# A fixed VectorE order and a fixed DMA order in the middle of a hybrid decoder layer

## The chip, the cores and the metric

The kernel runs on one core of a Trainium2 chip. The metric is the device time of one execution in microseconds (us). The engines of the core work side by side: TensorE (PE in the profile; PEld is its weight load), VectorE (DVE), ScalarE (ACT), GpSimd (POOL) and SyncE (SP), whose queue issues nearly all DMAs here. Each engine takes its instructions in the order in which the program gives them, and an instruction can wait for a semaphore of another engine.

## The reference, cut to what matters

The layer has a token-mixing part with three branches, then cross-attention and an MLP; the sequence and the width are both 1024. The change lies in the end of the token mixing.

```python
u = h @ w_in
dq, dk, dv, rq, rk, rv, rg, lx, ly, gates = split(u)
od  = diff_attention(...)                      # branch 0
o_r = silu(rg) * group_norm(retention(...))    # branch 1
hl  = rg_lru_branch(lx, ...)                   # branch 2
o_l = hl * gelu(ly)
g = sigmoid(gates)
merged = g[0]*(od @ w_branch[0]) + g[1]*(o_r @ w_branch[1]) + g[2]*(o_l @ w_branch[2])
x = x + merged @ w_out

def rg_lru_branch(xb):                         # per block of 128 channels
    xc = causal_conv(xb, width 4) + conv_b
    r, i = sigmoid(xc @ w_a + b_a), sigmoid(xc @ w_x + b_x)
    log_a = -8 * r * softplus(-lam)
    b = sqrt(-expm1(2*log_a)) * i * xc
    h[t] = exp(log_a[t]) * h[t-1] + b[t]
```

All is in float32; the kernel reaches that on TensorE by splitting each operand into an upper and a lower part and multiplying three times.

## The kernel before, in words

**Number format.** `split` (line 68) writes the upper part of an operand with a ScalarE copy (line 70) and the lower part with a subtraction on VectorE or GpSimd (line 71). `mm3` (lines 57 to 61) makes three matmuls of the upper and lower parts.

**Products.** The projections of the gates, of the silu input `rg`, of the LRU inputs and of the three branches are done with Strassen's scheme in Winograd's form: a pair of output tiles (two units of 128 channels, all 1024 positions) takes seven products of twelve 128x512 matmuls. `product` (line 1158) issues one product into one of six PSUM buffers (`p6`, line 751) and then whatever combination of products has become possible: `u2`, `u3` and the update behind `c22` (lines 1182, 1184, 1187) on VectorE, and `emit` for a finished quarter of the output. The order of the seven is `ORDER`, (1, 2, 6, 7, 5, 4, 3).

**Weights.** `ahead` (line 1143) runs `prep` some three products in front of the use: `pair_load` loads the two raw weight tiles (line 1128) into the pool `stage` of three buffers, or for odd pairs partly into a fixed tile, `left` (line 1117) makes the four sums of the scheme on VectorE, and `pair_unit` splits each left operand.

**Jobs.** `h_products` (line 664) runs 23 pairs one after the other: four `rg` pairs, eight `lru` pairs (at even places from 2 to 16) and eleven `gate` pairs. A `gate` pair stores its raw values (line 707) into the DRAM tensor `gsp`. An `rg` pair loads the retention output, applies silu and multiplies (lines 709 to 713). An `lru` pair ends in the convolution of four VectorE steps (lines 613 and 615, all of them behind its sixth product); in the next pair follow the split of the result (`xcs`) behind the sixth product and behind the seventh `lru_gate` (line 623): twelve matmuls, sigmoids into the tiles r and g, GpSimd's multiply (634), tanh, exp and square root (635 to 637) and four VectorE steps, of which line 640 is the scan, and the store of the block (642).

**Right operands of the branches.** `o_sums` (line 755) loads two rows of a branch's input into the same tiles r and g, makes four subtractions on VectorE (765) and stores the sums (767). The list `sums` says behind which pair each of the twelve turns stands, one or two to a pair.

**Branches.** `branch` (line 812) runs four pairs for each branch, the last two interleaved. Its `emit` loads the gate tile (822), takes the sigmoid (823), loads the partial sum of the branch before (826), does two or three VectorE steps (828, 829, 831) and stores the sum (833) or, for the last rows of the last branch, splits it for `w_out`. `load_blocks` and `fill_block` load and split the next branch's right operands (791); at the end of the third branch the first half of `w_o` is loaded in four pieces through one tile `wst` (880) and split, and the last block of the merged rows is filled.

**What sets the order.** The instructions are written in program order, but a planner sorts those of each engine by dependencies, priorities and its own durations. `after(key, ins)` (line 74) fixes the order of the instructions that carry the same key, without a semaphore; `wdma` and `hdma` are such keys for weight and block loads.

## Time and profile before

| | us |
|---|---|
| median of 3 runs | 2422.93 (2420.59 to 2424.95) |
| the profiled execution | 2424.15 |
| its span, first to last instruction | 2422.4 |
| TensorE busy | 2319.7 (96%) |
| VectorE busy | 1888.0 (78%) |
| ScalarE busy | 1041.4 (43%) |
| GpSimd busy | 955.9 (39%) |

The order of the stages on the span: retention and attention up to about 745 us, `h_products` from there to about 1252, the branches to about 1505, `w_out` behind them, then cross-attention and MLP. A row of the profile names the line, the engine, the operation, the tile written and those read; "x" gives a count, then come busy time, mean time of one in ns, and the idle time of the engine in front of it with what ended it. A row of waits gives who waited, for whom, us in total, times and the longest. A row of a stretch gives its bounds and length, then the busy time and number of instructions of PE, PEld, DVE, ACT and POOL, the granted TensorE clock (1.00 is full), the busy share of the DMA engines and GB/s. Matmuls are pipelined and their ends are modelled, so that their busy times overlap; starts are counted instead.

### The profile page before, as it was taken

Reading aid. Unit: us, or ns where it says so; the run is one execution under the profiler, and the core shown is the slowest. Engines: PE = TensorE matmul, PEld = TensorE weight load, DVE = VectorE, ACT = ScalarE, POOL = GpSimd, SP = SyncE. Lnnn points to the kernel's source line nnn. Section 1 sums busy time; section 2 is a strip of 40 time slices with the busy share of each in tenths; the row PEclk is TensorE's granted clock in tenths of the full one; section 3 lists DMA queues with packets and bytes.
Section 4 is the critical chain, followed back from the end, with each engine's and each line's share of the span. In section 5 each row is a group of like instructions: output and inputs, shape, how many; then the busy total and the mean of one; then the engine's idle time right before and its main releaser. Section 6 shows DMA issues by size and latency. Waiting matters only on the chain. (4 is left out here: it accounts for less than half of the span.)

```text
span 2422.4 us, 31108 instructions
## 1 busy us (share of the span) xinstructions
PE 2319.7 (96%) x11156; PEld 1913.1 (79%) x11156; DVE 1888.0 (78%) x2909; ACT 1041.4 (43%) x1817; POOL 955.9 (39%) x621
## 2 busy tenths in 40 slices
PE   9999999999999998999999988999989999899998
PEld 7888878888887876777887767778768888788886
DVE  7677487878797788798787898344788888788896
ACT  5443355555555543554354444135442222343333
POOL 1122212222215444455431223034155555598863
PEclk9999999999999999999999999999999999999999
DMA  5222122222215354543576687343225443744341
GB/s 173 81 87 70 58 70 60 64 71 70 62 49 180 127 162 162 174 134 136 178 266 240 228 287 239 105 146 119 97 83 183 152 144 135 254 167 166 121 165 70
DMA packets 135994, 335.12 MB, mean 138 GB/s; under 512 B 17040, under 2 KB 27281, under 8 KB 135840
## 3 DMA queue, kind: packets, MB, share of 16 engines
q1 hardware_dynamic: 135264, 331.30, 41.4%
q8 instruction: 89, 1.46, 0.2%
q10 hardware_dynamic: 576, 1.84, 0.2%
q14 instruction: 65, 0.53, 0.1%
HBM read 227.64 MB, written 97.05 MB: 134 GB/s over the span
## 5 line engine op out<-in xcount | busy, mean ns | idle before, releaser
L59 PE MATMUL ps<-block,wu 128*128 128x512 f32 x1428 | 568.6, 398 | 27.2 <-DVE sf L1187 10.4
L61 PE MATMUL ps<-block,wu 128*128 128x512 f32 x1428 | 565.3, 396 | 10.2 <-DVE wu L71 10.2
L60 PE MATMUL ps<-block,wu 128*128 128x512 f32 x1428 | 561.9, 394 | 0.8 <-DVE block L71 0.8
L71 POOL TENSOR_TENSOR wu<-st,wu 128x512 fp32r<-128x512 f32 x144 | 227.3, 1585 | 303.4 <-ACT wu L70 290.4
L59 PEld LDWEIGHTS ps<-block,wu 128*128 128x128 f32 x1428 | 272.4, 191 | 89.0 <-DVE sf L1187 11.3
L61 PEld LDWEIGHTS ps<-block,wu 128*128 128x128 f32 x1428 | 271.2, 190 | 75.1 <-DVE wu L71 13.3
L60 PEld LDWEIGHTS ps<-block,wu 128*128 128x128 f32 x1428 | 271.8, 190 | 61.0 <-DVE block L71 1.3
L70 ACT CAST wu<-st 128x512 fp32r<-128x512 f32 x240 | 141.9, 620 | 210.1 <-DVE st L1117 94.1
L71 POOL TENSOR_TENSOR w<-st,w 128x1024 fp32r<-128x1024 f32 x50 | 124.6, 2501 | 176.7 <-ACT w L70 176.5
L59 PE MATMUL ps<-wu,hu 128*128 128x512 f32 x456 | 179.4, 394 | 8.0 <-ACT wu L70 4.2
L60 PE MATMUL ps<-wu,hu 128*128 128x512 f32 x456 | 178.9, 392 | 0.9 <-POOL wu L71 0.8
L61 PE MATMUL ps<-wu,hu 128*128 128x512 f32 x456 | 178.6, 392 | 0.0
L71 POOL TENSOR_TENSOR wu<-sf,wu 128x512 fp32r<-128x512 f32 x63 | 122.2, 1954 | 131.9 <-ACT wu L70 95.8
L1273 DVE TENSOR_TENSOR acc<-acc,ps 128x512 f32<-128x512 f32 x184 | 118.1, 679 | 19.8 <-PE ps L61 19.4
L71 DVE TENSOR_TENSOR hu<-sth,hu 128x1024 fp32r<-128x1024 f32 x53 | 118.1, 2231 | 14.3 <-ACT hu L70 13.6
L466 ACT ACTIVATE p<-sc,mx 128x256 f32<-128x256 f32 (+7 forms) x128 | 94.8, 742 | 69.9 <-DVE mx L463 50.1
L71 DVE TENSOR_TENSOR wu<-st,wu 128x512 fp32r<-128x512 f32 x96 | 91.1, 960 | 30.9 <-ACT wu L70 30.8
L59 PEld LDWEIGHTS ps<-wu,hu 128*128 128x128 f32 x456 | 86.3, 189 | 28.7 <-ACT wu L70 4.6
L59 PE MATMUL psk<-block,w 128*128 128x512 f32 x256 | 101.6, 397 | 0.0
L60 PEld LDWEIGHTS ps<-wu,hu 128*128 128x128 f32 x456 | 86.3, 189 | 19.3 <-POOL wu L71 1.3
L61 PE MATMUL psk<-block,w 128*128 128x512 f32 x256 | 101.2, 395 | 0.0
L60 PE MATMUL psk<-block,w 128*128 128x512 f32 x256 | 100.8, 394 | 0.0
(383 smaller groups left out, 5627.4 us busy)
## 6 DMA issues: line engine op xcount, KB each, us to landing
sth<-h SPq DMA_DIRECT2D x53, 512.0 KB, 3.2
st<-in_w SPq DMA_DIRECT2D x32, 512.0 KB, 4.2
h<-hab SPq DMA_DIRECT2D x32, 512.0 KB, 2.8
w<-in_w SPq DMA_DIRECT2D x8, 2048.0 KB
block<-oTs SPq DMA_DIRECT2D x24, 512.0 KB, 5.8
sgb<-gsp SPq DMA_DIRECT2D x48, 256.0 KB, 5.3
gsp<-l SPq DMA_DIRECT2D x44, 256.0 KB, 2.8
acc<-y SPq DMA_DIRECT2D x40, 256.0 KB, 2.9
```

Source lines behind the costliest of these rows:

```text
L59: nc.tensor.matmul(ps, lhsT=lhs.hi, rhs=rhs.hi, start=start, stop=False)
L60: nc.tensor.matmul(ps, lhsT=lhs.hi, rhs=rhs.lo, start=False, stop=False)
L61: nc.tensor.matmul(ps, lhsT=lhs.lo, rhs=rhs.hi, start=False, stop=stop)
L70: ins = self.nc.scalar.copy(dst.hi, src)
L71: self.lo_ins = (lo_engine or self.nc.vector).tensor_tensor(dst.lo, src, f32(dst.hi), op=ALU.subtract)
L466: nc.scalar.activation(p[:, 0:n], sc[:, 0:n], AF.Exp, bias=mx, accum_out=l)
L1273: v.tensor_tensor(acc[k][:, st, :], acc[k][:, st, :], ps, op=ALU.add)
```

## The change

1. For pairs 2 to 20 of `h_products` each VectorE instruction is tied to the one before it in the program (`InOrder`), so that VectorE's order there is the program's.
2. The LRU work is cut into steps, at most one behind a product: the convolution behind the sixth and seventh product of its pair and the first two of the next, the split behind the third, the gate behind the fifth, and the four steps of the scan behind products two to five of the pair after that.
3. `o_sums` becomes a generator: loads behind the fifth product, its subtractions one to three at a time behind later products. The multiply and store of an `rg` quarter come two products later.
4. In the branches the loads of weights, blocks, gates and partial sums and the stores go in one order on SyncE (`one_queue`). Three gate tiles are loaded ahead, two are already through the sigmoid; partial sums are loaded ahead; each store is issued one emit later.
5. The weights of the next branch's first pair are loaded earlier, into a tile of the branch pool (`room`). `w_o` comes in two loads of two pieces, split behind products 7 and 3; the last block of the merged rows is split inside `w_out`.

No arithmetic is added or left out.

```diff
+class InOrder:
+    def __getattr__(self, name):
+        def issue(*args, **kw):
+            ins = getattr(self.engine, name)(*args, **kw)
+            if self.kernel.in_order:
+                self.kernel.after("dve", ins)
+            return ins
+        return issue
...
     def after(self, key, ins):
+        if self.one_queue and key in ("wdma", "hdma"):
+            key = "sp"
...
+    def lru_scan(self, n, c, step):
+        v, xc, gy, (r, g) = self.nc.vector, c["xc"], c["gy"], c["rg"]
+        if step == 0:
+            v.scalar_tensor_tensor(g, r, 1.0, g, op0=ALU.add, op1=ALU.mult)
+        elif step == 1:
+            v.tensor_tensor(xc, xc, g, op=ALU.mult)
+        elif step == 2:
+            v.tensor_tensor_scan(g, r, xc, 0.0, op0=ALU.mult, op1=ALU.add)
+        else:
+            v.tensor_tensor(gy, gy, g, op=ALU.mult)
+            self.nc.sync.dma_start(self.olT[n * P:(n + 1) * P, :], gy)
...
+            in_bw = bool(turns) and p >= m + 2
+            if in_bw:
+                at = 6
             if k == at and p == (turns or [p])[0] and q < len(pairs):
-                self.pair_load(q, *pairs[q])
+                self.pair_load(q, *pairs[q], self.bw.tile([P, 2, D], F32, tag="wst", name="wst") if in_bw else None)
...
-            if kind == "lru" and k == self.ORDER[5]:
-                self.lru_conv(n, c, sp)
...
+            if lru(p - 2) and 0 < at < 5:
+                self.lru_scan(jobs[p - 2][1], cs[p - 2], at - 1)
+            if lru(p) and at > 4:
+                self.lru_conv(n, c, sp, at - 5)
+            if lru(p - 1):
+                if at < 2:
+                    self.lru_conv(jobs[p - 1][1], cs[p - 1], sp, at + 2)
+                elif at == 2:
                     self.lru_split(cs[p - 1])
-                elif k == self.ORDER[6]:
+                elif at == 4:
                     self.lru_gate(jobs[p - 1][1], cs[p - 1], sp, sps)
-            if k == self.ORDER[2]:
-                for i, q in sums.get(p, ()):
-                    self.o_sums(i, q, sp)
+            if p in sums and at == 4:
+                self.steps = itertools.chain.from_iterable(self.o_sums(i, q, sp) for i, q in sums[p])
+                next(self.steps)
+            if p == m - 3 and p in sums:
+                count = {5: 2, 6: 2}.get(at, 0)
+            elif p in sums:
+                count = len(sums[p]) * (at == 6)
+            elif p < m - 2:
+                count = {0: {1: 1, 2: 3}, 1: {1: 1}, 2: {1: 1, 2: 2}, 3: {2: 2}}.get(at, {}).get(len(sums.get(p - 1, ())), 0)
...
+        def fetch():
+            if self.sg_line:
+                r, sl, i = self.sg_line.popleft()
+                sg = bw.tile([P, HB], F32, tag="sg", name="sgb", bufs=4)
+                self.after("sp", nc.sync.dma_start(sg, self.gsp[i * D + r * P:i * D + (r + 1) * P, sl]))
+                self.sgs.append([sg, False])
+            if self.pv_line and (len(self.sgs) > 2 or not self.sg_line):
+                at, r, sl = self.pv_line.popleft()
+                pv = None
+                if at > 0:
+                    pv = bw.tile([P, HB], F32, tag="pv", name="pv", bufs=3)
+                    self.after("sp", nc.sync.dma_start(pv, self.acc[at - 1][r * P:(r + 1) * P, sl]))
+                self.pvs.append(pv)
+            for g in [g for g in list(self.sgs)[:2] if not g[1]]:
+                g[1] = True
+                nc.scalar.activation(g[0], g[0], AF.Sigmoid)
+
+        def store(last=1):
+            while len(self.stores) > last:
+                self.after("sp", nc.sync.dma_start(*self.stores.popleft()))
...
-            if k in (7, 5, 3, 4):
-                if k in (7, 3):
-                    w.append(self.block(self.slotB))
-                q = units % 2
-                self.split(w[-1][:, 2 * q:2 * q + 2, :], wst, (v, nc.gpsimd)[q])
-                units += 1
+            if k in (7, 3):
+                w.append(self.block(self.slotB))
+                for q in range(2):
+                    self.split(w[-1][:, 2 * q:2 * q + 2, :], wst[:, q].rearrange("p (k c) -> p k c", k=2), (v, nc.gpsimd)[q])
+            if k in (1, 7):
+                wst = bw.tile([P, 2, D], F32, tag="wst", name="wst")
+                for q in range(2):
+                    self.after("sp", nc.sync.dma_start(wst[:, q], self.a["w_o"][0, (0 if k == 1 else 2) + q]))
...
+                    if half == 0 and j == 1 and cb == 1:
+                        self.fill_block()
```

More of the change, by code (lines that the diff above doesn't have):

```diff
@@ L1 @@
 import collections
+import itertools
 from contextlib import ExitStack
@@ L667, in h_products @@
             pairs += [(b[p], [a["w_br"][i * 8 + 2 * p + e] for e in range(2)]) for p in range(4)]
+        puts = collections.deque()
         def prep(p, k):
@@ L716, in run @@
             self.product(k, c, H, psum or self.p6(sps), emit)
-            if kind == "lru" and k == self.ORDER[5]:
-                self.lru_conv(n, c, sp)
             if p == 1 and k == 3:
                 self.softplus()
-            if p > 0 and jobs[p - 1][0] == "lru":
-                if k == self.ORDER[5]:
+            for x in puts:
+                x[0] -= 1
+            while puts and puts[0][0] == 0:
+                puts.popleft()[1]()
+            at = self.ORDER.index(k)
+            lru = lambda q: 0 <= q < m and jobs[q][0] == "lru"
@@ L730, in h_products @@
+            if p == m - 3 and p in sums:
[4 more added lines that the diff above has]
+                count = {0: {1: 1, 2: 3}, 1: {1: 1}, 2: {1: 1, 2: 2}, 3: {2: 2}}.get(at, {}).get(len(sums.get(p - 1, ())), 0)
+            else:
+                count = 0
+            for _ in range(count):
+                next(self.steps)
         for p in range(2):
@@ L832, in emit @@
             if nxt is not None or n < 4:
-                nc.sync.dma_start(self.acc[order][rows, sl], o)
+                self.stores.append((self.acc[order][rows, sl], o))
             else:
                 self.split(mT[j][1][:, n % 4, :], o)
+            store()
+            fetch()
         def run(p, k):
@@ L866, in branch @@
             elif k in (2, 3):
+                store(0)
                 j = 3 - k
@@ L1122, in left, with raw_pair @@
         raw.update(S1=s1, S2=s2, S4=s4, S3=raw["A21"])
-    def raw_pair(self, units, second=None):
+    def raw_pair(self, units, second=None, first=None):
         raw = {}
         for i, unit in enumerate(units):
-            st = second if i and second is not None else self.stage.tile([P, D], F32, tag="st", name="st")
+            st = (first, second)[i]
+            if st is None:
+                st = self.stage.tile([P, D], F32, tag="st", name="st")
             self.after("wdma", self.nc.sync.dma_start(st, unit))
```

81 lines of the change are left out of this document (55 added, 26 removed).

## The prediction

> **What bounds the kernel now.** I read the page's first part, then the stretches that the change touches, cut by TensorE's rhythm.
>
> ```profile
> PE 2319.7 (96%) x11156; PEld 1913.1 (79%) x11156; DVE 1888.0 (78%) x2909; ACT 1041.4 (43%) x1817; POOL 955.9 (39%) x621
> ...
> 860.00:1180.00 320.00, 294.63 (x1232) 236.64 (x1231) 270.82 (x282) 152.99 (x216) 158.61 (x88) 0.97 0.44 149
> 1180.00:1320.00 140.00, 140.00 (x615) 114.96 (x614) 108.72 (x136) 62.08 (x93) 38.57 (x27) 1.00 0.69 239
> 1320.00:1460.00 140.00, 126.42 (x524) 101.39 (x523) 124.85 (x166) 63.63 (x97) 34.42 (x18) 0.94 0.79 262
> 1460.00:1500.00 40.00, 40.00 (x176) 32.86 (x175) 37.33 (x46) 18.27 (x29) 14.69 (x8) 1.00 0.67 224
> 1500.00:1540.00 40.00, 28.22 (x107) 21.10 (x106) 25.98 (x28) 12.26 (x19) 11.31 (x6) 0.79 0.49 161
> ```
>
> TensorE sets the end, so a gain is a matmul that starts earlier. From 1180 to 1320 us nothing holds it: 615 matmuls in 140 us, 0.2276 us each; a product of twelve takes 2.73 us. At that rate 860 to 1180 (the pairs with an LRU block) has 1232 x 0.2276 = 280.4 us of work in 320, so 39.6 are lost; 1320 to 1460 (branches) loses 140 - 119.3 = 20.7; 1500 to 1540 (end of the third branch, first output rows) loses 40 - 24.4 = 15.6; 1180 to 1320 and 1460 to 1500 lose nothing. So 75.9 us lie within reach, and the forecast is how much of them returns.
>
> What TensorE waited for in the three losing stretches, in this order (waiter, releaser: us, times, longest), and the clock behind two stalls:
>
> ```profile
> PE psr L60 <- DVE xcs L71: 11.0, 6, 2.6
> PE ps L59 <- DVE sf L1187: 10.4, 5, 3.6
> PE ps L61 <- DVE wu L71: 3.9, 2, 3.3
> ...
> PE ps L59 <- ACT wu L70: 9.8, 3, 6.7
> PE ps L61 <- DVE wu L71: 3.7, 3, 2.9
> ...
> PE pso L59 <- ACT block L70: 9.1, 2, 5.7
> ...
> 957.40:959.70 2.30, 0.48 (x3) 0.05 (x2) 2.30 (x4) 1.11 (x3) 0.42 (x1) 1.00 0.87 244
> 959.70:963.10 3.40, 3.40 (x9) 2.62 (x10) 3.31 (x4) 1.07 (x3) 3.40 (x3) 0.52 0.68 264
> ```
>
> In the LRU stretch every wait is for VectorE: the lower half of the LRU input (xcs), a PSUM bank not read yet (L1187), a weight's lower half. They sum to 25.3 of 39.6 us. Part of the rest is the clock: behind the stall at 957 nine matmuls start in 3.4 us at a granted 0.52, where 15 would.
>
> Is VectorE late by order or by amount? One LRU block takes a cycle of two pairs, 14 products and a gate's 12 matmuls, 15 x 2.73 = 41.0 us. The cycles, cut where each stores its result (columns: PE, PEld, DVE, ACT, POOL busy):
>
> ```profile
> 847.30:895.70 48.40, 46.15 (x199) 36.84 (x197) 39.55 (x44) 25.69 (x36) 22.64 (x14) 1.00 0.44 139
> 895.70:945.40 49.70, 42.40 (x176) 33.80 (x177) 41.88 (x44) 21.98 (x31) 23.07 (x14) 0.97 0.48 162
> 945.40:993.60 48.20, 44.31 (x179) 35.45 (x178) 41.34 (x44) 22.10 (x31) 22.05 (x13) 0.93 0.49 166
> 993.60:1042.30 48.70, 43.32 (x180) 34.63 (x179) 41.86 (x45) 21.99 (x31) 23.34 (x14) 0.96 0.49 166
> 1042.30:1083.10 40.80, 39.35 (x172) 31.93 (x172) 37.27 (x40) 22.08 (x31) 22.74 (x14) 1.00 0.43 146
> 1083.10:1132.00 48.90, 45.71 (x194) 37.07 (x193) 41.84 (x44) 22.11 (x31) 23.48 (x14) 0.97 0.46 155
> 1132.00:1172.70 40.70, 38.79 (x163) 31.34 (x162) 34.98 (x37) 20.42 (x28) 22.53 (x12) 0.96 0.30 105
> ```
>
> By both. Two cycles already run at 40.7 and 40.8. Five take 48.2 to 49.7, 243.9 us together; four of these carry two o_sums, and VectorE is busy 41.3 to 41.9 us in them, more than TensorE needs. No order brings those under about 41.9.
>
> **Part 1, VectorE in program order, one LRU step a product.** No instruction is added or removed; the order is a constraint without a semaphore. Its durations over the LRU stretch (us busy, mean ns):
>
> ```profile
> L71 DVE TENSOR_TENSOR wu<-st,wu 128x512 fp32r<-128x512 f32 x29 | 35.6, 1242 | 20.2 <-ACT wu L70 20.2
> L693 DVE TENSOR_TENSOR l<-ps,sf 128x512 f32<-128x512 f32 x45 | 30.7, 681 | 4.3 <-DMA gsp<-l 3.8 <-PE ps L61 0.3
> L615 DVE SCALAR_TENSOR_TENSOR xc<-lx,vec,xc 128x1024 f32<-128x1024 f32 x21 | 27.2, 1297 | 0.1
> L640 DVE TENSOR_TENSOR_SCAN g<-r,xc 128x1024 f32<-128x1024 f32 x7 | 22.5, 3213 | 0.0
> L1117 DVE TENSOR_TENSOR st<-st 128x512 f32<-128x512 f32 x21 | 17.4, 828 | 0.6
> L765 DVE TENSOR_TENSOR r<-g,r 128x512 f32<-128x512 f32 x11 | 10.7, 975 | 2.3 <-DMA g<-olT 2.3
> ...
> L71 DVE TENSOR_TENSOR xcs<-xc,xcs 128x1024 fp32r<-128x1024 f32 x7 | 9.5, 1357 | 0.0
> ```
>
> I lay them on the new order, taking 0.68 for each of seven combines a pair, 1.24 for a weight's lower half (two a pair), 0.83 for each of the four left-hand sums (3.3), 1.30 for a convolution step, 1.36 for xcs, 3.21 for the scan and 1.30 for the other three steps, 0.8 for an o_sums step. The LRU pair's seven slots then hold 0, 2.0, 2.0, 3.9, 3.9, 6.5, 3.6 us; the pair behind it 2.9, 2.0, 3.6, 2.3, 2.6, 5.2, 0.7. That is 41.2 against 41.0 of TensorE, level with the measured 41.9, so the estimate holds. Letting 2.73 a slot drain, VectorE's queue starts empty, is 1.2, 2.3, 6.1 and 7.0 us deep from the fourth slot on, 6.4 to 7.3 in the next pair's first four slots and 4.5 at its end, which the next cycle's first three slots drain. PSUM's six banks give some five products, 13.7 us, so the L1187 wait goes. The gate stands two products, 5.5 us, behind xcs; 7.3 us deep less two o_sums steps of 0.8 puts xcs 5.7 us behind its product, and a stop of VectorE ahead of it adds to that: 0 to 3 us of stall remain, I take 1.5.
>
> What the fixed order blocks: an instruction that waits now holds all of VectorE, the combines behind it and so PSUM. The worst place is the second o_sums of a cycle, which loads into the same tiles r and g. Both halves of that turn stand in the list of DMA issues (KB each, median us to landing), and SyncE's wait ahead of such loads in its list of waits:
>
> ```profile
> oTs<-g SPq DMA_DIRECT2D x9, 512.0 KB, 2.8
> g<-orT SPq DMA_DIRECT2D x4, 512.0 KB, 4.3
> ...
> SPq L762 <- DVE g L640: 72.0, 6, 13.0
> ```
>
> Store 2.8 plus load 4.3 is 7.1 us behind the first one's last step; the order puts 2.0 + 0.7 + 1.4 + 0.8 = 4.9 us of work between. VectorE stands still for some 2.2 us, more if SyncE is held. The 72.0 us are SyncE standing at o_sums loads whose tiles the scan still uses, with weight loads behind them; the new place of these loads, behind the block's last LRU step, shortens that, and the block's own store goes ahead of them. I take 2.6 for this and the smaller waits. So a cycle of two sums becomes 40.9 + 1.5 + 2.6 = 45.0, the first (39.55 us busy, one sum) 41.3, the two clean ones stay: 41.3 + 4 x 45.0 = 221.3 against 243.9, **minus 22.6 us**. Ends: minus 36.2 if each of the five falls to the larger of 40.8 and its VectorE time (207.7), and minus 7 if the first alone heals.
>
> A gate two products earlier needs r and g free earlier. In the trace ScalarE loses time on just that:
>
> ```profile
> ACT L633 <- DMA oTs<-r: 18.3, 2, 9.2
> ```
>
> In the new order the store of r also precedes the gate; I count no gain, its price is in the 2.6. The delayed multiply and store of the silu pairs is hidden: its result is read a pair later.
>
> The Trainium skill (TensorE: Matmul & The Clock Gate, Part 1) has the clock fall after an idle window of about 3.4 us. By that the stalls of 1.5 us left over cost nothing more; the trace shows half clock behind a 2.2 us stall, and if each of four did that, 6 matmuls x 0.2276 = 1.4 us each, the sum would lose 5.5.
>
> **Part 2, branches: one order on SyncE, early gates, stores one emit late.** Between 1255 and 1500 us ScalarE and SyncE waited:
>
> ```profile
> ACT sgb L823 <- DMA sgb<-gsp: 56.4, 25, 7.0
> ...
> SPq L833 <- DVE y L829: 51.9, 14, 8.0
> SPq L833 <- DVE y L831: 48.7, 22, 6.6
> ```
>
> SyncE spends 100.6 us of 245 in front of stores of unfinished results, with loads behind them. ScalarE spends 56.4 before gate tiles, with the weight casts behind, and the casts are what TensorE waits for (9.8). Three gate tiles in hand are some three emits of 7/4 products, 14 us, against a longest wait of 7.0 in the row; a store one emit late is nearly always ready. Both waits shrink to little. The next branch's first weights come eight products earlier, into a tile of their own. Not cured: at a boundary ScalarE also waits for blocks, whose slots come free only with TensorE's last use. Of the 20.7 us (13.5 waits, the rest clock) I take **14 back**; ends 20.7 and minus 3, should a load that waits for its slot now hold gates and stores behind it.
>
> **Part 3, output weights and the last block.** Of w_o's four pieces through one tile, the last is cast and split here:
>
> ```profile
> 1514.80 1.04 ACT L70 CAST block<-wst 128x1024 fp32r<-128x1024 f32 x1
> ...
> 1515.92 2.86 POOL L71 TENSOR_TENSOR block<-wst,block 128x1024 fp32r<-128x1024 f32 x1 [2.23 <-ACT block L70]
> ```
>
> TensorE stood until 1518.8 for that (5.7 of the 9.1 us above, then 2.1). Two loads of two pieces put the last split before the last two products, and the last block's split goes behind w_out's first rows. What is late next is the third branch's own result: its emits still run to the end on VectorE. I take **9 of 15.6**; ends 15.6 and 0.
>
> **Sum.** The profiled execution took 2424.15 us (span 2422.4, 1.75 around it; the runs' median is 1.2 lower). 2424.15 - 22.6 - 14 - 9 = 2378.6; I say **2379**. All best ends: 2424.15 - 36.2 - 20.7 - 15.6 = 2351.7. All low ends short of a loss, 7 + 6 + 6: 2405.
>
> **Rivals.** (A) The LRU cycles stay at 48 to 49: the slowness is VectorE beside GpSimd, not order. For it: a weight's lower half takes 1.24 us on average, a combine that reads PSUM 0.68 for the same size, and GpSimd is busy 23 us of each cycle. Against: the clean cycles have the same 22.7 of GpSimd and run at 40.8. It gives 2424.15 - 14 - 9 = 2401. The Trainium skill (SBUF — State Buffer, Who interferes with whom) has VectorE instructions with two SBUF inputs and GpSimd exclude each other, which is such a mechanism.
> (B) SyncE's fixed order clogs behind a load that waits for a slot: parts 2 and 3 give nothing, 2424.15 - 22.6 = 2401.5. For: SyncE waits already. Against: the stores, its longest waits there, are the ones moved.
> (C) Slower. VectorE blocks in the fixed order at the second o_sums and at the scan's first step, whose square root comes late when ScalarE stands before r. A cycle has 48.8 - 41.9 = 6.9 us of room, and 23 us from the branches pay 5.8 more in four cycles: above 12.7 us of standing still per cycle the kernel is slower. At 15 it takes 2424.15 - 23 + 4 x 8.1 = 2433.6. Against: a wait of 2.2 is what the landings give.
> (D) No change: the order differs on paper, and the stalls move by as much as they shrink, 2423.
>
> **Chances.** Forecast 0.62 (its own range 2352 to 2405), A 0.12, B 0.08, C 0.11, D 0.07. This measurement can tell about 0.2%, 4.8 us: faster 0.82, within it 0.07, slower 0.11. For 8 in 10 the range runs from 2353 to 2421, which leaves out C, D and a little below.
>
> **What would show it.** Part 1 right: TensorE's waits for xcs and L1187 under 5 us together, the five cycles at 41 to 46, VectorE's busy time per cycle unchanged; wrong: VectorE's waits for loads of r and g above 10 us a cycle. Part 2 right: ScalarE's wait for gates under 15 us, 1320 to 1460 of the old stretch with over 570 matmuls in 140 us; wrong: new SyncE waits for slots. Part 3 right: no wait for the cast of wst. The whole is wrong if the LRU cycles still take 48.

## The result, and the profile after

The changed kernel takes 2438.99 us (median of 4 runs, 2437.81 to 2439.07) beside 2421.76 for the kernel before (4 runs on the same chip, 2418.4 to 2424.95): a ratio of 1.0067, with a 95% interval of 1.0054 to 1.008. It is slower by 17 us where 44 us of gain were forecast, and outside the range.

The head of the profile's page after, and its first part (busy time and share by engine):

```profile
span 2435.9 us, 31134 instructions
...
PE 2320.2 (95%) x11156; PEld 1908.9 (78%) x11156; DVE 1853.1 (76%) x2909; ACT 1049.4 (43%) x1825; POOL 945.2 (39%) x621
```

TensorE, VectorE and GpSimd run as many instructions as before; ScalarE runs eight more, all of them loads of its function tables (48 beside 40, 1.28 us each). VectorE is even busy 35 us less than before. The span is 13.5 us longer. Cut at the first matmul of each stage, by the two traces (here and below a stage's length is that of one execution; the executions of one kernel spread by up to 12 us, as the ten of `e1` below do, from 2424.0 to 2435.9):

| stage | before, us | after, us | difference |
|---|---|---|---|
| to the first product | 722.4 | 722.3 | -0.1 |
| 23 pairs (LRU, gates, silu) | 524.4 | 535.0 | +10.6 |
| branch 0 | 76.8 | 83.5 | +6.7 |
| branch 1 | 86.3 | 87.8 | +1.5 |
| branch 2 | 87.8 | 86.7 | -1.1 |
| w_out | 110.9 | 109.1 | -1.8 |
| cross-attention | 160.5 | 160.6 | +0.1 |
| MLP | 653.3 | 650.9 | -2.4 |

The loss sits in the two places from which 36.6 of the 45.6 us of gain were to come.

**The LRU cycles**, cut from one store of a block's result to the next as in the prediction (bounds, length, then busy time and number of PE, PEld, DVE, ACT, POOL, granted clock, DMA share, GB/s):

```profile
845.40:895.00 49.60, 44.53 (x178) 35.11 (x177) 37.87 (x44) 31.01 (x40) 23.34 (x13) 0.93 0.42 147
895.00:943.50 48.50, 44.06 (x188) 34.69 (x187) 37.21 (x44) 21.96 (x31) 20.71 (x13) 1.00 0.47 156
943.50:993.90 50.40, 44.05 (x182) 34.68 (x181) 37.58 (x44) 21.96 (x31) 21.01 (x13) 0.97 0.46 160
993.90:1043.60 49.70, 43.82 (x182) 34.57 (x182) 37.42 (x44) 21.96 (x31) 20.55 (x13) 0.97 0.47 161
1043.60:1087.90 44.30, 41.94 (x182) 33.88 (x181) 34.51 (x40) 22.05 (x31) 19.37 (x13) 1.00 0.43 146
1087.90:1138.70 50.80, 43.88 (x180) 34.50 (x179) 37.85 (x44) 21.94 (x31) 20.53 (x13) 0.97 0.43 145
1138.70:1179.30 40.60, 39.84 (x174) 32.40 (x173) 33.01 (x36) 19.65 (x28) 19.13 (x11) 1.00 0.36 112
```

Five cycles of 48.2 to 49.7 us became five of 48.5 to 50.8, and the one with a single turn of `o_sums` that took 40.8 takes 44.3. VectorE's busy time in the cycles with two turns of `o_sums` fell from 41.3 to 41.9 us to 37.2 to 37.9, and they grew longer. So VectorE's amount does not set them. What the engines waited for from 820 to 1180 us, in the list of waits after (TensorE, VectorE, ScalarE):

```profile
PE psr L88 <- ACT xcs L99: 13.2, 6, 3.2
PE ps L90 <- POOL wu L100: 11.8, 12, 2.4
PE psr L89 <- DVE xcs L59: 4.9, 6, 1.3
...
DVE l L59 <- ACT sf L1299: 26.4, 7, 9.2
DVE g L59 <- ACT g L670: 23.8, 4, 6.8
DVE l L59 <- ACT l L758: 15.1, 2, 7.8
...
ACT xcs L99 <- DVE xc L59: 48.4, 7, 8.8
ACT L666 <- DMA oTs<-r: 15.2, 3, 5.4
```

TensorE's wait for a PSUM bank (L1187 before, 10.4 us) is gone, as forecast. In its place stand waits for the LRU's split, now through ScalarE's cast, and for GpSimd's lower halves. VectorE now stands 65.3 us behind ScalarE: for the copy of product 1 (L1299), for the square root (L670) and for silu (L758). And ScalarE stands 48.4 us behind VectorE's convolution. Before, in the same stretch, VectorE waited for next to nothing of ScalarE's but weight casts (0.7 us for silu), and ScalarE less for the convolution:

```profile
DVE wu L71 <- ACT wu L70: 22.6, 7, 4.8
...
ACT xcs L70 <- DVE xc L615: 13.1, 5, 2.7
```

Two queues that each work in order hold one another. One cycle in the timeline after (start, length, instruction, idle time before it and what ended it):

```profile
1009.20 1.04 ACT L99 CAST xcs<-xc 128x1024 fp32r<-128x1024 f32 x1 [8.81 <-DVE xc L59]
...
1020.60 1.28 ACT L666 ACT_TABLE_LOAD   x1 [5.13 <-DMA oTs<-r]
...
1032.26 1.06 ACT L670 ACTIVATE g<-g 128x1024 f32<-128x1024 f32 x1
...
1033.35 1.23 DVE L59 SCALAR_TENSOR_TENSOR g<-r,g 128x1024 f32<-128x1024 f32 x1 [6.79 <-ACT g L670]
```

Read downward, it is the loop: the cast of the split waits for the convolution, the gate's sigmoid for the store of the sums out of r, the square root begins 11.7 us behind the sigmoid's table load, and VectorE has stood for 6.79 us at the scan's first step when it arrives.

**The branches.** The list of waits after from 1255 to 1515 us (SPq is SyncE's queue of DMAs, L915 the store of a partial sum):

```profile
ACT sgb L911 <- DMA sgb<-gsp: 68.1, 31, 6.2
...
SPq L915 <- DVE y L59: 121.0, 34, 9.3
...
PE ps L90 <- DVE wu L59: 6.2, 1, 6.2
PE ps L88 <- ACT block L99: 5.9, 2, 3.2
PE ps L89 <- DVE block L59: 4.2, 3, 2.8
PE ps L88 <- ACT wu L99: 1.0, 1, 1.0
```

Both waits that were to shrink grew: ScalarE's for gates from 56.4 to 68.1, SyncE's in front of stores from 100.6 to 121.0. TensorE's own waits went from 13.5 to 17.3 us. At the start of branch 0 SyncE's queue shows what the order does (timeline after):

```profile
1261.93 4.30 SPq L754 DMA_DIRECT2D gsp<-l  x2
1267.93 1.27 SPq L900 DMA_DIRECT2D sgb<-gsp  x3
1269.30 0.90 SPq L867 DMA_DIRECT2D block<-orT  x2
```

The first three gate loads stand behind the last stores of gates, and the last right block of branch 1, whose load before was issued at 1249.6 and 1252.9 us, stands behind them at 1269.3. TensorE came to that block at 1273.5 us and stood until 1277.1; the matmuls behind that stall took 0.63 to 0.80 us instead of 0.39.

**The start of w_out.** One row of the list of waits after, 1500 to 1625 us:

```profile
PE pso L88 <- DVE xt L59: 8.5, 1, 8.5
```

and the timeline around it:

```profile
1533.27 0.62 ACT L99 CAST block<-y 128x512 fp32r<-128x512 f32 x1 [1.38 <-DVE y L59]
1533.28 2.06 ACTq L1014 DMA_DIRECT2D xt<-in_x  x2
...
1538.00 0.69 DVE L59 TENSOR_TENSOR xt<-xt,pso 128x512 f32<-128x512 f32 x1 [3.02 <-DMA xt<-in_x]
```

Before, TensorE waited 11.2 us for blocks there: 5.7 for ScalarE's cast of `w_o` and 2.1 for GpSimd's lower half of it, and 3.5 for the cast of the third branch's own result. The two for `w_o` are gone. What is late now is the load of the residual rows: ScalarE issues it, behind its cast of the third branch's last result, and VectorE's addition, which frees the PSUM bank, waits for its landing. Before, ScalarE issued that load behind the same cast (at 1519.4 us), but TensorE stood until 1518.8 us for `w_o` then, and no wait of TensorE's for a bank shows.

### The profile page after: what moved, and what is told of

It reads as the page before. It is cut to its first block, busy times and chain, and to the rows that moved or that the text cites. A ratio compares the mean times of both kernels' runs of the same rounds, so it can differ in the third digit from the quotient of the medians.

```text
span 2435.9 us, 31134 instructions
## 1 busy us (share of the span) xinstructions
PE 2320.2 (95%) x11156; PEld 1908.9 (78%) x11156; DVE 1853.1 (76%) x2909; ACT 1049.4 (43%) x1825; POOL 945.2 (39%) x621
## 5 line engine op out<-in xcount | busy, mean ns | idle before, releaser
L90 PE MATMUL ps<-block,wu 128*128 128x512 f32 x1428 | 565.8, 396 | 20.5 <-POOL wu L100 11.8
L90 PEld LDWEIGHTS ps<-block,wu 128*128 128x128 f32 x1428 | 271.2, 190 | 87.3 <-POOL wu L100 16.9
L99 ACT CAST wu<-st 128x512 fp32r<-128x512 f32 x232 | 135.8, 618 | 219.0 <-DVE st L59 116.1
L59 DVE TENSOR_TENSOR acc<-acc,ps 128x512 f32<-128x512 f32 x200 | 128.4, 677 | 19.8 <-PE ps L90 19.5
L100 POOL TENSOR_TENSOR wu<-sf,wu 128x512 fp32r<-128x512 f32 x61 | 104.5, 1730 | 90.5 <-ACT wu L99 75.6
L59 DVE TENSOR_TENSOR hu<-sth,hu 128x1024 fp32r<-128x1024 f32 x53 | 116.4, 2198 | 12.5 <-ACT hu L99 12.0
L88 PEld LDWEIGHTS ps<-wu,hu 128*128 128x128 f32 x456 | 86.0, 189 | 27.1 <-DVE acc L59 3.9
L89 PEld LDWEIGHTS ps<-wu,hu 128*128 128x128 f32 x456 | 86.0, 189 | 19.5 <-POOL wu L100 1.4
L90 PEld LDWEIGHTS ps<-wu,hu 128*128 128x128 f32 x456 | 86.0, 189 | 18.1
```

Source lines behind the costliest of these rows:

```text
L59: ins = getattr(self.engine, name)(*args, **kw)
L88: nc.tensor.matmul(ps, lhsT=lhs.hi, rhs=rhs.hi, start=start, stop=False)
L89: nc.tensor.matmul(ps, lhsT=lhs.hi, rhs=rhs.lo, start=False, stop=False)
L90: nc.tensor.matmul(ps, lhsT=lhs.lo, rhs=rhs.hi, start=False, stop=stop)
L99: ins = self.nc.scalar.copy(dst.hi, src)
L100: self.lo_ins = (lo_engine or self.nc.vector).tensor_tensor(dst.lo, src, f32(dst.hi), op=ALU.subtract)
```

## The experiments

The medians of the kernel before that stand beside the runs lie between 2420.37 and 2423.73 us. Ratios are to the kernel before on the same chip, with 95% intervals; where two runs stand beside different medians of it, their distances to these are compared.

**The two halves apart.** `e1_lru_new` has the new LRU part and the branches of before; `e2_branches_new` the LRU part of before and the new branches.

```diff
 # e1 (on the changed kernel; emit, stores and w_out as before)
-            in_bw = bool(turns) and p >= m + 2
+            in_bw = False
 # e2 (on the kernel before): the changed branch(), one_queue, room and w_out
```

> The new LRU and gate part (VectorE tied, steps spread) with the branches, the output weights and the last block as they were. The trace of the changed kernel puts the end of the last gate store 13 us later than before and the start of the output rows 4 to 5 us later still, of which 2 to 4 come back behind it. Theory L (the LRU part is the loss: its cycles stay bound by the round trip of the tiles r and g, and the fixed order adds standing still): 2422 + 13 = 2435, between 2431 and 2439. Rival Q (the loss is in the branches' fixed queue order, and the LRU part only looks later): 2420 to 2426.

> The LRU and gate part as it was, with the new branches (one order on SyncE, early gates, late stores, weights in a tile of their own, output weights in two loads, the last block split later). Theory L: the branches change little, since the 6.8 us that TensorE newly loses at their start eat what the rest wins: 2420 to 2426. Rival Q: 2431 to 2439. If the two parts add up, this run and the one with the LRU part alone give 2439 together: their differences from the kernel before sum to 17 us.

Measured: e1 2430.11 us (1.0031, 1.0018 to 1.0044), e2 2425.34 (1.0007, 0.9995 to 1.0019). The LRU half is slower by itself, the branch half gives nothing. Beside 2422.32 they cost 7.8 and 3.0 us, 10.8 of the 17. Most of what is left is branch 0: it takes 76.8 us in e1, 78.0 in e2 and 83.5 with both.

**What the fixed order of VectorE costs.** The order that ties each VectorE instruction to the one before it is called the tie from here on. `e3_untied` drops it and keeps all else; `e7_scan_untied` frees the four scan steps alone.

```diff
 # e3
-        self.in_order = True
 # e7
-        v, xc, gy, (r, g) = self.nc.vector, c["xc"], c["gy"], c["rg"]
+        v, xc, gy, (r, g) = self.nc.nc.vector, c["xc"], c["gy"], c["rg"]
```

> The changed kernel without the tie of VectorE's instructions; the steps stay spread, the planner orders them. Theory T (the tie itself makes VectorE wait for ScalarE's square root and copies, 26.4 + 23.8 + 15.1 us in the trace): 2424 to 2431, about 10 us back of 17. Theory L with the loop alone as the bound: the loop of r and g is as long either way, 2436 to 2441.

> The changed kernel with the four LRU scan steps left out of the tie, the rest of VectorE tied. Theory S (the tie costs because VectorE stands at the scan's first step until ScalarE's square root is done, 23.8 us in four cycles): most of the 12 us that the whole tie costs come back, 2427 to 2431. Rival: the tie costs at other places (VectorE behind ScalarE's copies and silu, 26.4 and 15.1 us): 2435 to 2441.

Measured: e3 2427.03 us (1.0014, 1.0003 to 1.0025), e7 2432.9 (1.0055, 1.0037 to 1.0073). So the changed kernel's 17.2 us above the one before become 4.7 without the tie and 12.5 with the scan alone freed: some 12 of the 17 are the tie. In e3 the 23 pairs take 524.9 us, as in the kernel before (524.4), beside 535.0 with the tie. Without the tie no copy of product 1 appears among VectorE's waits.

**Is a cycle bound by a loop or by VectorE's amount?** `e4_one_sum_before` spreads the twelve turns of the sums, one to a pair as far as they go, in the kernel before; `e5_one_sum_after` does so in the changed kernel; in `e8_no_second_load` the second turn of a cycle skips its loads, so that a DMA's time leaves the cycle and VectorE's work stays (what that turn stores is not what the branches need).

```diff
 # e4, e5
-        sums = {4: [(0, 0)], 6: [(1, 0), (1, 1)], 8: [(1, 2), (1, 3)], 10: [(0, 1), (0, 2)], 12: [(0, 3)],
-                14: [(2, 0), (2, 1)], 18: [(2, 2)], 20: [(2, 3)]}
+        sums = {4: [(0, 0)], 6: [(1, 0)], 8: [(1, 1)], 10: [(1, 2)], 12: [(1, 3)], 14: [(0, 1)], 16: [(2, 0), (0, 2)],
+                18: [(2, 1), (2, 2)], 19: [(0, 3), (2, 3)]}
 # e5 also
-            elif p in sums:
+            elif p in sums and at > 3:
...
 # e8, in o_sums
-        for e in range(2):
+        for e in range(0 if again else 2):
```

> The kernel before with the o_sums turns spread: one turn in each LRU cycle but the last, the other five behind the LRU blocks, where r and g are free. Nothing is left out. Theory L (cycles of two turns are 8 us longer because r and g go round once more): the four such cycles fall from 48.8 to about 41, 2422 - 4 x 7.5 = 2392, between 2388 and 2402. Rival V (the cycles are bound by VectorE's amount): it also falls, by the 3.2 us of a turn in each of four cycles, of which the late turns give nothing back: 2405 to 2412. A rival by which neither matters: 2420 to 2424.

> The kernel before, in which the second o_sums turn of a cycle makes its subtractions and stores on the data that are in the tiles already: four times two loads are left out, the VectorE work stays the same; what it stores is not the sums that the branches need. Theory L (latency of the round trip bounds the cycles of two turns): each falls by about a load, 3.2 to 4.4 us, 2422 - 15 = 2407, between 2403 and 2412. Rival V (VectorE's amount bounds them): 2419 to 2424.

> The changed kernel with the o_sums turns spread, one to an LRU cycle but the last, the other five behind the LRU blocks. Nothing is left out. Theory L: four cycles fall from 49.9 to the 44.3 of its one cycle with one turn, 2439 - 22 = 2417, between 2412 and 2424; it stays some 9 us behind the kernel before with the same turns (2408), since a cycle with one turn takes 44.3 here and about 41 there. Rival T (the tie makes VectorE stand still whatever the turns): 2430 to 2439.

Measured: e4 2408.42 us (0.9935, 0.9918 to 0.9951), e8 2409.15 (0.9952, 0.9937 to 0.9967), e5 2436.24 (1.0058, 1.0042 to 1.0073). Three cycles of e4, second to fourth:

```profile
895.40:937.80 42.40, 38.60 (x165) 30.97 (x166) 37.60 (x40) 22.06 (x31) 23.23 (x14) 1.00 0.41 139
937.80:978.20 40.40, 40.40 (x178) 33.09 (x177) 36.75 (x40) 22.17 (x31) 21.75 (x13) 1.00 0.44 146
978.20:1019.20 41.00, 41.00 (x181) 33.58 (x180) 37.37 (x41) 22.16 (x31) 22.95 (x14) 1.00 0.42 145
```

and the third and fourth of e8:

```profile
939.80:985.40 45.60, 42.89 (x181) 34.77 (x180) 41.32 (x44) 22.48 (x31) 22.64 (x14) 0.96 0.45 154
985.40:1029.60 44.20, 41.84 (x183) 33.98 (x182) 41.44 (x44) 22.59 (x31) 23.06 (x14) 1.00 0.46 157
```

One turn fewer shortens a cycle by 7.3 to 7.8 us though VectorE's busy time in it falls by 4.3 to 4.6, and in e8 the cycles with VectorE busy 41.3 and 41.4 us, as before, run 2.6 and 4.5 us faster. By its time alone e4 lies in the range of the rival by which VectorE's amount counts, and outside the one expected; the cycles and e8 speak for the other reading. The cycle of before is a round trip through the one pair of tiles r and g: gate, scan, two turns of load, subtraction and store, next gate. The stage is shorter by 22 us in e4, and 7 of them are lost again behind it: branch 0 takes 83.9 us there instead of 76.8. In the changed kernel the same spread brings the two-turn cycles from 49.9 to some 43.5 us too, but the turns moved to the last pairs cost most of it again (the last cycle grows from 40.6 to 49.4 us, and the stage ends 5 us earlier), and nothing that can be told is left at the end: the expected gain of 22 us did not come.

**A gate moved ahead in the fixed order.** `f1_gate_earlier` runs one turn to a cycle, two convolution steps to a product, and split and gate two products earlier. Of its edit only the place of split and gate is shown.

```diff
-                if at < 2:
-                    self.lru_conv(jobs[p - 1][1], cs[p - 1], sp, at + 2)
-                elif at == 2:
+                if at == 0:
                     self.lru_split(cs[p - 1])
-                elif at == 4:
+                elif at == 2:
                     self.lru_gate(jobs[p - 1][1], cs[p - 1], sp, sps)
```

> The changed kernel with the o_sums turns spread, one to an LRU cycle, the convolution's steps two behind a product instead of one, and split and gate two products earlier (behind products one and three of the next pair). VectorE stays tied. Theory G (in the tied order a cycle is the way once round: convolution, split, gate, ScalarE's sigmoid to square root, scan, and VectorE idles some 6.7 us of each while ScalarE is at tanh, exp and square root, since gate and scan stand too close): the cycles fall from 43.5 with one turn to about 41, 2436 - 17 = 2419, between 2412 and 2426. Rival (the tied order stands still wherever the gate is placed): 43 to 44 a cycle, 2430 to 2439.

Measured: 2471.19 us (1.0205, 1.0185 to 1.0225), far above both ranges. The list of waits of this run, 820 to 1180 us:

```profile
ACT g L666 <- DMA oTs<-g: 24.8, 5, 6.4
...
DVE l L59 <- ACT sf L1298: 50.4, 6, 9.3
...
PE ps L88 <- ACT wu L99: 16.8, 7, 3.1
PE psr L88 <- ACT xcs L99: 14.5, 7, 4.4
```

The gate's sigmoids stand in ScalarE's queue for the sums' store, and everything written behind them stands too: the copy of product 1, for which VectorE now waits 50.4 us, and the weight casts, for which TensorE waits. Read from these waits, an early place in the program does not make the gate early; it blocks a queue early. The three parts of the edit were not run apart.

**Is it the tiles r and g, or the order?** In these runs the sums of `o` take a slot of the weights' ring (the tiles `w`, which also hold the split weights and the split `xcs` of the LRU's input) in place of r and g: `g1_own_before` on the kernel before, `g2_own_after` on the changed one, `g5_own_untied` on e3. `h2_steps_untied` is g2 with the LRU's steps and the sums out of the tie; the products' additions and the weights' sums stay in it.

```diff
 # g1, g2, g5
-        t = [sp.tile([P, 2, HB], F32, tag=t, name=t) for t in "rg"]
+        t = f32(self.wpool.tile([P, 2, 2, HB], F32R, tag="w", name="os"))
+        t = [t[:, e] for e in range(2)]
 # h2: lru_conv, lru_split, lru_scan and o_sums use self.nc.nc.vector
```

> The kernel before; the column sums of o take one slot of the weights' ring instead of the tiles r and g. Nothing is left out, and VectorE's amount of work is the same. Theory L (a two-turn cycle is the round trip through the single pair r and g: gate, scan, two turns of the sums, next gate): the sums no longer stand in it, so the two-turn cycles fall from 48.8 us to the 41 to 43 us that the cycles with one turn or none show, some 10 us of them come back in branch 0 as in the run with one turn a cycle, and the kernel takes 2403 to 2412 us. Rival V (the cycle is set by VectorE's and GpSimd's amount of work): the cycles stay at 48 to 49 us and the kernel at 2418 to 2424 us. Rival W (the ring of weights, now used once more in a turn, is what the products wait for): cycles over 49 us, 2425 us or more.

> The changed kernel with the same edit: the sums of o in a slot of the weights' ring, the fixed order of VectorE kept. Theory K (the tie is dear only through the shared pair r and g, since ScalarE stands before r and g for the stores of the sums while VectorE stands behind ScalarE): the cycles fall to 42 to 45 us like those of the kernel before with this edit, the kernel takes 2415 to 2423 us, and its distance to the kernel before with the same edit is 10 to 13 us, all of it in the branches. Theory F (a fixed order of VectorE is dear by itself, whatever it waits for): the cycles stay at 47 us or more or at least 3 us above those of the kernel before with the same edit, and the distance between the two stays 17 us or grows.

> The changed kernel with the sums in a slot of their own and without the fixed order of VectorE. Theory K: the tie costs nothing once the pair r and g is free of the sums, so this run lies within 3 us of the one with the tie. Theory F: it lies 8 to 14 us below it, as the two runs without the edit do (2427.0 beside 2439.0 us).

> The changed kernel with the sums of o in a slot of the weights' ring (2427.0 us), and the LRU's own steps (convolution, split, scan, column sums) no longer tied; the products' additions and the weights' sums keep their fixed order. Theory X (the price of the tie is that two streams of work, one waiting for ScalarE and one for TensorE and the loads, stand in one line): it falls to 2407 to 2414 us, nearly the 2408.0 us of the run with nothing tied, and cycles of 42 to 44 us. Rival Y (the order among the products and the weights is what costs): it stays at 2420 us or more, cycles of 46 us or more.

Measured: g1 2409.11 us (0.9949, 0.9931 to 0.9967), g2 2427.04 (1.0013, 1.0002 to 1.0024), g5 2407.98 (0.9935, 0.9918 to 0.9952), h2 2425.26 (1.0015, 1.0005 to 1.0025). The loop is real: breaking it brings 14.6 us to the kernel before, 13.9 to the changed one and 20.5 to e3, with no work added or left out. In the changed kernel TensorE waited 11.8 us for GpSimd; that wait is 0.6 in g2. But the tie's price does not go with it: g2 lies 19 us above g5, more than the 12 between the changed kernel and e3. My theory that the tie is dear only through r and g fell. TensorE's waits in g2 from 840 to 1180 us,

```profile
PE psr L88 <- ACT xcs L99: 12.5, 5, 4.4
PE psr L89 <- DVE xcs L59: 3.6, 6, 1.3
PE ps L88 <- ACT wu L99: 1.8, 1, 1.8
PE ps L90 <- POOL wu L100: 0.6, 1, 0.6
```

beside those in g5:

```profile
PE psr L89 <- DVE xcs L59: 10.4, 4, 4.2
PE psr L88 <- ACT xcs L99: 2.0, 2, 1.4
```

With the tie, the gate's matmuls find the split late in six cycles. Without it they wait for it in four. In g2 the new slot is itself shared: ScalarE's cast of the split waits for the sums' stores out of the ring,

```profile
ACT xcs L99 <- DMA oTs<-os: 26.8, 4, 8.2
```

beside 4.0 us in g5. The stage's difference is 16.9 us, between two executions that lie 26 us apart where the medians lie 19. TensorE's waits of these rows differ by 6.1, and the clock takes an estimated 5 (five cycles of g2 ran at 0.93 to 0.96 of full speed and three of g5 at 0.92 to 0.96, the others at 1.00; the missing share times the length is 13.6 us beside 8.5). The rest, some 6, stands in no one row. Freeing the LRU's own steps and the sums (h2) brings nothing that the measurement can tell (3.5 us above the kernel before, where g2 is 3.3), though the split's wait for the ring is gone there (weight casts wait 10.5 us for it, 11.0 in g5); so the shared ring alone is not the price. As far as this one run tells, the price lies in what stays tied, the order among the products' additions and the weights' sums. The last column of the LRU's input `lx` is among these, and the convolution waits for it (ScalarE waits 32.1 us for `xc` in h2, beside 9.6 in g5). Which pairs of instructions are the dear ones was not separated.

**The order on SyncE.** `e6_block_first` puts the last right block's load ahead of the first gates in the changed kernel. On e2, `f4_own_queues` gives weights, blocks and gates back their own orders, and `f2_late_stores` puts the block first and issues each store two outputs late instead of one.

```diff
 # e6, f2
                 if (p, k) == (0, 1):
                     next(self.loading)
+                    if order == 0:
+                        for _ in range(3):
+                            fetch()
 # f2
-        def store(last=1):
+        def store(last=2):
 # f4
-            self.one_queue = True
```

> The changed kernel with the first three gate loads of the branches issued behind the last right block's load instead of ahead of it. Theory H (the fixed order of SyncE puts gate loads, which wait for the last gate store, ahead of a block that TensorE needs first): the first branch falls from 83.5 to about 78 us, 2439 - 6 = 2433. Rival: the block is late because ScalarE and VectorE are late from the LRU part: no change, 2437 to 2441.

> The old LRU and gate part with the new branches, in which weights and blocks keep their own orders and only gates, partial sums and late stores share one: the planner mixes the three on SyncE. Theory H (the single order costs by putting block and weight loads behind stores and gates): 2416 to 2422 against 2425 with the single order. Rival (the single order is not what costs): 2424 to 2428.

> The old LRU and gate part with the new branches, in which the first gate loads come behind the last right block's load and each store is issued two emits late instead of one. Theory H (the fixed order makes blocks wait behind stores whose data VectorE has not made: 121 us of SyncE's waits, none fewer than the 100.6 before): with later stores the blocks come earlier and the three branches, 256.7 us from first product to first output row with the stores one emit late, fall to 246 to 250: 2425 - 8 = 2417, between 2413 and 2421. Rival (the blocks are late because their slots and the DMA engines come free late): 2422 to 2428.

Measured: e6 2433.12 us (1.0053, 1.0036 to 1.0071), f4 2421.39 (0.9997, 0.9986 to 1.0008), f2 2417.21 (0.9977, 0.9967 to 0.9988). In e6 branch 0 is back at 76.8 us: its 6.7 us of loss were the block behind the gates. Branch 1 takes 91.0 us in that execution instead of 87.8, and the kernel's median gains 4.5, with intervals that overlap. f4 lies 3.4 us below e2, which the two intervals do not tell from nothing. The three branches took 250.9 us before, 256.7 in e2, 254.9 in f4 and 248.7 in f2. f2's list of waits, 1250 to 1500 us:

```profile
SPq L830 <- DVE y L852: 96.7, 32, 11.2
```

SyncE no longer stands at stores; it stands nearly as long at the loads of gates, whose four slots are taken. f2 lies 7.6 us below e2. Of the 8.0 us that its branches win, 1.2 are branch 0, where the block stood behind the gates; the rest is put down to the stores, since e6, with the block first alone, keeps 119.0 us of SyncE's waits in front of stores.

**What the runs add up to.** `f3_best` is f2 with the spread turns of e4, `g3_own_late` f2 with the sums in a slot of the ring, `h1_untied_late` the changed kernel untied, with the sums in a slot of the ring, block first and stores two outputs late. Their edits are those above.

> The old LRU part with the o_sums turns spread, one to a cycle but the last, and the branches with the first gates behind the block and stores two emits late. If both edits work and add up: 2408 - 8 = 2400, between 2396 and 2406; if the branches' edit gives nothing: 2408 to 2412.

> The LRU part of the kernel before with the new branches, the last right block's load ahead of the first gates, stores two outputs late (2417.2 us in its run), and the sums of o in a slot of the weights' ring. Theory L: the gain of the edit adds to it, 2400 to 2408 us, the fastest version so far or level with the one that spreads the turns (2404.8 us). Rival V: 2414 to 2419 us.

> The changed kernel without the fixed order of VectorE, the sums in a slot of their own, the last right block's load ahead of the first gates, and stores two outputs late. If the parts add up: the LRU part ends at 1227.7 us as in the run with nothing tied, and the three branches take the 248.7 us that they took with late stores instead of 256.5, so 2400 us. If the branches only pass on their waits, as they did in part in the runs before: 2404 to 2409 us.

Measured: f3 2404.8 us (0.9926, 0.9909 to 0.9943), g3 2407.93 (0.9936, 0.9914 to 0.9957), h1 2399.02 (0.991, 0.9895 to 0.9925). h1 is the fastest: 23 us below the kernel before and 40 below the changed one, with the program of the change and without its fixed order on VectorE. In g3 the parts do not add (late stores bring 1 us over g1); in h1 they do, 7 us over g5.

## Why the prediction was wrong, point by point

**What bounds the kernel.** That TensorE sets the end and loses its time in those three stretches held: nearly all that the runs gained came from them. The answer "By both" to the question whether order or amount makes VectorE late was the wrong reading of the cycles: e8 shortened cycles with VectorE's busy time unchanged, and e4 by more than the work that it took out. "No order brings those under about 41.9" was not refuted: the shortest cycle with two turns, in g5, takes 42.0 us. The cycle of 40.8 us that the forecast calls clean has one turn; only that of 40.7 has none. The sign that the forecast set for its own failure came: the LRU cycles still take 48 us and more.

**Part 1** (minus 22.6, measured plus 10.6) failed at the step that lays VectorE's work on product slots and lets 2.73 us of it drain in each. That treats VectorE as a queue that never waits, with 2.2 us of standing for the second `o_sums` and the rest "in the 2.6". Measured, it stands 65.3 us behind ScalarE alone in 360 us, some 9 a cycle of two pairs, and e3 shows that the loss of this part goes with the fixed order. The waits for loads of r and g, which I did price, come to 9.8 us in all that stretch. What I did not price is ScalarE's order: the copy of product 1 and the square root are written behind the gate, the gate waits for the sums' stores, and VectorE, tied, waits behind both. The row for it was quoted (ScalarE before r, 18.3 us) and then waved through with "I count no gain". TensorE's wait for a PSUM bank (L1187) went as said. The split's stall, taken as 1.5 a cycle, is 18.1 us over seven cycles, 2.6 each.

**Part 2** (minus 14, measured plus 7.1 over three branches) failed at "a store one emit late is nearly always ready": the wait for unfinished results grew by 20 us, and only two emits late took SyncE off the stores. It failed too at pricing the moved loads by the gates alone. The case that I kept as the low end, "should a load that waits for its slot now hold gates and stores", came, with other tenants: a gate load that waits for a store held a block, and that is 6.7 us. The step that fixes the order was never priced by who else stands in that queue. The sum's low end of 2405 takes 6 us each from parts 2 and 3 without a source; with the low ends that these parts name, minus 3 and 0, it would be about 2420, and still below the result.

**Part 3** (minus 9, measured minus 1.8): TensorE's waits for casts and lower halves of blocks went from 11.2 us to 3.0. "What is late next is the third branch's own result" named the right neighbour without a price; behind it, on ScalarE's queue, stands the load of the residual rows, and the 8.5 us there took back nearly all. The same wait is 7.6 in f2 and in h1, which have the new `w_out` too, and is not in e1, which has the old one; a run with that load elsewhere was not made, so its cause is read from the timeline only.

**Rivals.** C (slower, 2433.6) was right in kind: VectorE blocked at the scan's first step, 23.8 us, because ScalarE stood before r. It had the wrong size, since the largest single wait, the copy of product 1, is in neither the forecast nor the rival, and its bar of 12.7 us of standing a cycle counted 23 us from parts 2 and 3 that did not come. By its own bar, some 9 us a cycle behind ScalarE would have left the kernel faster, so that its figure lies 5 us from the result is luck. A (VectorE beside GpSimd) explains durations, not the cycles: VectorE's busy time fell by 4 us a cycle, and the cycles grew. B (the order on SyncE clogs) was true of the branches, and stopped short of a loss. D was not the case.

## What to carry to other kernels

Before fixing an engine's order, follow each instruction in it to its releaser, and that releaser's own queue: where two engines in fixed orders wait for each other, amounts of work and a drained queue say nothing, the round trip does. A tile pair shared by two users is a loop, and its length is read from stores and loads as much as from engines; moving one user to a slot of another ring was worth 11 to 20 us here, though that ring has users too, and the fixed order cost 12 to 19. When a stall is cured, look at what the next instruction on the same queues waits for, DMA issues on a compute engine's queue among them.

## What the hardware showed that was not expected

**VectorE's busy time is no fixed amount.** Groups of instructions on VectorE after, 860 to 1180 us (busy us, mean ns of one, idle time before):

```profile
L59 DVE TENSOR_TENSOR l<-ps,sf 128x512 f32<-128x512 f32 x41 | 27.8, 683 | 31.2 <-ACT sf L1299 26.1 <-PE ps L90 2.6 <-DMA orT<-l 2.1
L59 DVE TENSOR_TENSOR wu<-st,wu 128x512 fp32r<-128x512 f32 x28 | 24.6, 878 | 0.0
```

A weight's lower half went from 1262 ns in the same stretch before to 878, the scan from 3213 to 2665, while the addition that reads PSUM stayed at 0.68 us. Sorting the records of this stretch by whether a GpSimd instruction overlaps them: the lower half takes 683 ns alone (14 of them) and 1842 beside GpSimd (14) in the trace of before, 677 (20) and 1380 (8) after; the addition with one source in PSUM takes 0.68 us either way. Fewer of these instructions fall beside GpSimd after the change, so at least part of VectorE's 35 us less of busy time is less of this slowing, and not less work. The Trainium skill (SBUF — State Buffer, Who interferes with whom) says that a VectorE instruction with two SBUF inputs contends with a GpSimd instruction that reads SBUF, and one with at most one, outside the two-port modes, does not; the trace agrees, with the numbers above.

**The clock behind a stall.** Stretches after: a stall of TensorE and the 3.4 us behind it, twice.

```profile
957.00:959.90 2.90, 0.00 (x0) 0.00 (x0) 2.31 (x4) 1.09 (x2) 0.10 (x1) 1.00 0.77 222
959.90:963.30 3.40, 2.87 (x11) 2.07 (x12) 2.08 (x2) 1.51 (x3) 1.79 (x1) 1.00 0.91 348
...
1530.30:1538.70 8.40, 0.00 (x0) 0.00 (x0) 5.36 (x7) 2.18 (x3) 0.00 (x0) 0.62 0.59 233
1538.70:1542.10 3.40, 3.36 (x8) 2.69 (x9) 0.69 (x1) 0.00 (x0) 0.00 (x0) 0.50 0.00 0
```

Behind 2.9 us the clock stayed at 1.00; behind 8.4 us it was 0.50 for 3.4 us, with 8 matmul starts where the next 3.4 us have 15. In the trace of before a stall of some 2 us (957.4 to 959.7 us) was followed by 0.52. So a stall's length alone does not tell what the clock adds to it. The clock rule that the prediction took from the Trainium skill (TensorE: Matmul & The Clock Gate, Part 1) fits the two stalls here and not the one before.
